# Two-block network on one core: query scaling, ready biases, early constants, a fourth weight buffer

## The chip, the cores and the metric

The kernel runs on one core of a Trainium2 chip, in one launch. The metric is the device time of an execution in microseconds. Most executions of one kernel agree within 0.3%.

## The reference

The input is 256 tokens of width 1024, one batch. The reference is two blocks of two layers each, all in float32.

- The first block. Layer 0: a norm, an input projection, a short causal convolution, a 4-head mLSTM and 4-head attention over 256 memory tokens, then an output projection and a gated feed-forward with a 3-tap convolution. Layer 1: 12-head banded attention with a table of relative biases, again with memory attention, output projection and feed-forward. It ends in a norm with the gain `final_g`.
- The second block. Each of its layers is modulated: `mod = silu(c) @ ada_w + ada_b` gives shifts, scales and gates. The even layer mixes 8-head neighbourhood attention over a grid with a bias table `rpb` (plus all 256 context keys) and HGRN2, a gated linear recurrence that runs in both directions. The odd layer is a gated short convolution. Each is followed by a feed-forward with 2816 hidden features; a norm ends it.

Every attention computes `softmax(scale * q k + bias)` with `scale = 64 ** -0.5 = 1/8`:

```
s = einsum('bqhd,bkhd->bhqk', qc, kc) * scale + bias
p = softmax(where(valid, s, -inf))
```

## The kernel before

**Layout and products.** Activations lie with features on the partitions, 8 tiles of 128 features by 256 tokens. Float32 products are made from two halves: each operand is split into a high part and the rest, and each 128 x 128 weight tile needs three matmuls (high x high, high x low, low x high: L122 to L124 in `mm3`). Down projections use a wider form (L129, L130 in `mm2`). A projection of 8 k tiles is 24 matmuls of 256 (or 258) columns.

**Weights.** `load_w` loads 512 KB into a raw tile (4 buffers `wraw`), through SyncE's queue; ScalarE casts the high half (L114), VectorE subtracts for the low half (L115), into one of 3 buffers `w`. `out_proj` runs 8 projections; where it is given a pool and two tags, its fourth weight (`nt == 3`) goes into two dead tiles of that pool instead (`wspare`). Before the change the two output projections of the second block do this and those of the first block don't.

**PSUM.** Projections rotate over five banks (`acc` 3, `sc` 2) in wide stages and over three in others; VectorE evacuates them, mostly times the norm's `rstd`. A norm is: a sum of squares, a product with ones, a power on GpSimd (`inv_rms`, L224), transposes that spread it (L218), and a copy to `rstd`.

**Order.** A planner orders the instructions of every engine with simulated times, taking ready work in program order; `issue_after` puts one instruction behind another in its engine's queue. Each engine, and SyncE's load queue, then runs its list in order. A pool that is closed gives its bytes to the next pool opened at the same place; in a pool with `reuse_waits="tile"` a tile waits for the readers and writers of the old tiles under it.

**Modulation.** 96 steps `ada` each load 512 KB and make one reduction on VectorE (L469; 16 of them two). `ada_after` puts a step behind an evacuation; `ada_done` forces those that are needed. The pair `rates` of a feed-forward gives a step after every so many up tiles, and how many after each down tile.

**Around the change.** `Pair.scores` makes the scores of two heads: L332 computes `(score + bias) * -0.125` and the running minimum, so the biases are made 8 times as large before: for the band on GpSimd at L883 after its load at L882; for the neighbourhood at L1177, with the window mask `win` added at L1179. At the entry to the second block's first mixer (`mix2`, from L943) the pool's constants for HGRN2 are made on GpSimd and VectorE: `reset` (L974, L975), the masks `mf` and `mk` (L981, L984), `decay` (L988), `win` (L1153 to L1158). Just before, x is multiplied by `final_g` (L938, 8 instructions), which only the evacuations of that mixer's output projection need. The kernel begins with 16 matmuls on ones (L262) and with the loads of `memx` and of the memory keys' weights (L272, L273).

Of the kernel before, what the change touches and what calls it, by code (L numbers as in the profile page):

```python
# [9 lines left out]
F32 = mybir.dt.float32  # L10
# [42 lines left out]
def network(ctx: ExitStack, tc: tile.TileContext, a):  # L53
# [205 lines left out]

    ps = bank("fil")  # L260
# [40 lines left out]
    class Pair:  # L301
# [7 lines left out]
        def scores(self):  # L309
# [6 lines left out]
            for qts in ((0, 1),) if one else ((0,), (1,)):  # L316
# [9 lines left out]
                for qt, j in [(qt, j) for qt in qts for j in range(2)]:  # L326
# [3 lines left out]
                    for lo, n, b in self.bias(j, qt):  # L330
# [3 lines left out]
                            scale=-0.125, scalar=3e38 if mn is None else mn, op0=ALU.add,  # L334
# [198 lines left out]
    with tc.tile_pool(name="mix0", bufs=1, reuse_waits="tile") as pool:  # L533
        def scaled(ps, out):
            nc.vector.tensor_tensor(out=out, in0=ps[:, :S], in1=rstd[:, :S], op=ALU.mult)

        cm = pool.tile([P, S], F32, name="cm")
# [5 lines left out]
        qk = pool.tile([P, 12, S], F32, name="qk")  # L543

        qz = pool.tile([P, 4, S], F32, name="qz")
        nc.gpsimd.memset(qz, 0.0)

        def qk_step(nt):
# [17 lines left out]
            return nc.scalar.activation(qk[:, nt], cv, AF.Silu)  # L566
# [77 lines left out]
        def lstm_scores(h):  # L644
# [3 lines left out]
            parts = ((own, qk[:, own]), (shared, qz[:, h]))  # L648
# [11 lines left out]
            for i, (kt, q) in enumerate(parts):  # L660
                nc.tensor.matmul(sp[:, :S], qk[:, 6 + kt, 0:P], q, start=i == 0, stop=i == 1)
            for i, (kt, q) in enumerate(parts):
                nc.tensor.matmul(sp[:, S:384], qk[:, 6 + kt, P:S], q[:, P:S],
                                 start=i == 0, stop=i == 1)
# [26 lines left out]
        def mem_q(nt):  # L691
            scaled(proj_fm(a["w_qm0"][nt], x2), qm[:, nt])
# [46 lines left out]
        out_proj(a["w_aout"], y2, (6, 7, 0, 1, 2, 3, 4, 5), evac)  # L739
# [42 lines left out]
    with tc.tile_pool(name="mix1", bufs=1, reuse_waits="tile") as pool:  # L782
        kk = pool.tile([P, 6, S], F32, name="kk")
        vv = pool.tile([P, 2, 768], F32, name="vvb")
        qq = pool.tile([P, 6, S], F32, name="qq")
# [77 lines left out]
        def q_step(nt):  # L863
            scaled(proj_fm(a["w_bq"][nt], x2), qq[:, nt] if nt < 6 else qm[:, nt - 6])

        def k_step(nt):
            scaled(proj_fm(a["w_kvk"][nt], kv2), kk[:, nt])
# [11 lines left out]
        def band_pair(pair):  # L879
            def prep():  # L880
                relb = pool.tile([P, 2, S], F32, tag="relb", bufs=2, name="relb")
                nc.gpsimd.dma_start(out=relb, in_=a["rel"][pair])  # L882
                nc.gpsimd.tensor_scalar(out=relb, in0=relb, scalar1=8.0, scalar2=1.0,  # L883
                                        op0=ALU.mult, op1=ALU.mult)
# [4 lines left out]
                pool, qq[:, pair],  # L889
                lambda nk: [(0, nk, kk[:, pair, :nk])],  # L890
# [23 lines left out]
        out_proj(a["w_bout"], y2, (6, 7, 0, 1, 2, 3, 4, 5), evac)  # L914
# [22 lines left out]
    for kt in range(KT):  # L937
        nc.vector.scalar_tensor_tensor(out=x[:, kt], in0=x[:, kt], scalar=col("final_g", kt),  # L938
                                       in1=rx[:, :S], op0=ALU.mult, op1=ALU.mult)

    NM = S + 2
    with tc.tile_pool(name="mix2", bufs=1, reuse_waits="tile") as pool:
# [30 lines left out]
        reset = pool.tile([P, 8, 32], F32, name="reset")  # L973
        nc.gpsimd.memset(reset, 1.0)  # L974
        nc.gpsimd.memset(reset[:, :, 0:1], 0.0)  # L975
        resetf = reset.rearrange("p a b -> p (a b)")

        mk = pool.tile([P, 2, 2, P], U8, name="mk")
        mf = pool.tile([P, 2, 2, P], F32, tag="at", bufs=2, name="mf")
        for d, sgn in ((0, 1), (1, -1)):  # L980
            nc.gpsimd.affine_select(out=mf[:, d, 0], in_=ones, compare_op=ALU.is_ge, fill=0.0, base=0,  # L981
                                    pattern=[[sgn, P]], channel_multiplier=-sgn)
            for tb in range(2):
                nc.vector.tensor_copy(mk[:, d, tb], mf[:, d, 0])  # L984


        decay = pool.tile([P, 4, 2, 5], F32, name="decay")
        nc.gpsimd.memset(decay, 1.0)  # L988
# [161 lines left out]


        win = pool.tile([P, 64], F32, name="win")
        nc.gpsimd.memset(win, 0.0)  # L1153
        for half in range(2):
            hs = slice(64 * half, 64 * half + 64)
            nc.gpsimd.affine_select(out=win[hs, 0:48], in_=win[hs, 0:48], compare_op=ALU.is_ge,
                                    fill=NEG, base=8, pattern=[[1, 48]], channel_multiplier=-1)
# [44 lines left out]
        with tc.issue_after(sigmoid.ins):  # L1202
            for head in heads:
                head.logs()
# [216 lines left out]
```

## Time and profile before

| what | us |
|---|---|
| median of the runs shown | 1366.92 |
| lowest | 1364.28 |
| highest (one run of three, far off the others) | 3344.76 |
| the profiled execution | 1365.22 |
| its span, first to last instruction | 1363.5 |
| TensorE busy in it | 1338.8 (98%) |
| VectorE busy | 1118.2 (82%) |
| ScalarE busy | 830.1 (61%) |
| GpSimd busy | 49.1 (4%) |
| mean granted TensorE clock | 0.997 of full speed |

PE is TensorE (PEld its weight loads), DVE VectorE, ACT ScalarE, POOL GpSimd, SPq SyncE's queue of loads. A matmul's end in the trace is modelled and overlaps the next one; the number of matmuls in a stretch says more than the busy time.

### The profile page before, as it was taken

The page shows a single profiled execution, that of the slowest core. Times are in us where ns is not written, and L with a number is a line of the kernel's source. Part 1 is how long each engine was busy: PE and PEld are TensorE (multiplying, and loading weights), DVE is VectorE, ACT ScalarE, POOL GpSimd, SP SyncE. Part 2 cuts the span into 40 slices and gives each one's busy share as a digit, 9 for nine tenths or more (in the row PEclk, how much of TensorE's full clock was granted, in tenths as well). Part 3 has the DMA queues.
Part 4 walks back from the last instruction along what each step waited for, and adds up shares of the span by engine and source line. Part 5 has one row for each costly group of instructions (what it writes and reads, how often), then busy time and mean ns, then how long its engine had stood idle before and what let it go on. Part 6 is the DMA issues. An engine that isn't in the chain of part 4 may idle for free.

```text
span 1363.5 us, 26870 instructions
## 1 busy us (share of the span) xinstructions
PE 1338.8 (98%) x10498; PEld 1282.0 (94%) x10498; DVE 1118.2 (82%) x2121; ACT 830.1 (61%) x1440; POOL 49.1 (4%) x72
## 2 busy tenths in 40 slices
PE   9999999999999999999999999999999999999997
PEld 8998999989999999999888987999998999999986
DVE  6887799997775968998988876699889898888854
ACT  6856655555567766555647766576654455666653
POOL 1000000000101000000040110000000000000000
PEclk9999999999999999999999999999999999999999
DMA  7753677766645657888875443467779876655563
GB/s 272 246 176 105 230 231 228 235 202 191 213 148 155 209 201 242 283 283 277 269 229 173 151 153 123 139 232 230 224 216 339 284 244 195 186 177 181 176 187 100
DMA packets 80352, 284.19 MB, mean 208 GB/s; under 512 B 8928, under 2 KB 10080, under 8 KB 80096
## 3 DMA queue, kind: packets, MB, share of 16 engines
q1 hardware_dynamic: 79136, 278.67, 63.9%
q0 software_dynamic: 800, 3.15, 0.7%
q8 instruction: 82, 1.34, 0.4%
q10 hardware_dynamic: 288, 0.66, 0.1%
q14 instruction: 46, 0.38, 0.1%
HBM read 281.39 MB, written 1.05 MB: 207 GB/s over the span
## 4 chain that ended last, share of the span: by engine, by line
PE 93%; DVE 3%; ACT 2%; issue 1%; DMA 0%; POOLq 0%; POOL 0%; DVEq 0%; SPq 0%; ACTq 0%
PE ps_acc L124 15%; PE ps_acc L122 15%; PE ps_acc L123 15%; PE ps_sc L124 7%; PE ps_sc L123 7%; PE ps_sc L122 7%; PE ps_acc L129 6%; PE ps_sc L129 4%; PE ps_acc L130 3%; PE ps_sc L130 2%; PE ps_sc L323 2%; PE ps_acc L154 2%; PE ps_acc L156 2%; PE ps_acc L155 2%; DVE w L115 1%
## 5 line engine op out<-in xcount | busy, mean ns | idle before, releaser
L114 ACT CAST w<-wraw 128x1024 fp32r<-128x1024 f32 (+3 forms) x434 | 443.5, 1027 | 390.3 <-PE ps_acc L124 146.3
L115 DVE TENSOR_TENSOR w<-wraw,w 128x1024 fp32r<-128x1024 f32 (+3 forms) x434 | 519.9, 1201 | 120.5 <-ACT w L114 117.2
L124 PE MATMUL ps_acc<-x,w 128*128 128x258 f32 (+1 forms) x1576 | 446.5, 285 | 2.1 <-DVE w L115 2.1
L122 PE MATMUL ps_acc<-x,w 128*128 128x258 f32 (+1 forms) x1576 | 444.8, 285 | 3.7 <-DVE ev L947 1.6
L123 PE MATMUL ps_acc<-x,w 128*128 128x258 f32 (+1 forms) x1576 | 446.3, 284 | 0.0
L122 PEld LDWEIGHTS ps_acc<-x,w 128*128 128x128 f32 x1576 | 298.5, 190 | 7.9 <-ACT w L114 2.4
L124 PEld LDWEIGHTS ps_acc<-x,w 128*128 128x128 f32 x1576 | 298.9, 190 | 3.9 <-DVE w L115 2.5
L123 PEld LDWEIGHTS ps_acc<-x,w 128*128 128x128 f32 x1576 | 299.3, 190 | 2.3 <-issue 2.0
L122 PE MATMUL ps_sc<-x,w 128*128 128x256 f32 (+1 forms) x824 | 232.6, 282 | 1.9 <-ACT w L114 1.1
L124 PE MATMUL ps_sc<-x,w 128*128 128x256 f32 (+1 forms) x824 | 233.2, 283 | 0.0
L123 PE MATMUL ps_sc<-x,w 128*128 128x256 f32 (+1 forms) x824 | 232.6, 283 | 0.0
L122 PEld LDWEIGHTS ps_sc<-x,w 128*128 128x128 f32 x824 | 156.0, 189 | 2.9 <-ACT w L114 1.5
L123 PEld LDWEIGHTS ps_sc<-x,w 128*128 128x128 f32 x824 | 155.6, 189 | 0.4 <-issue 0.4
L124 PEld LDWEIGHTS ps_sc<-x,w 128*128 128x128 f32 x824 | 155.9, 189 | 0.1
L129 PE MATMUL ps_acc<-a,w 128*128 128x512 f32 x352 | 123.0, 390 | 0.0
L469 DVE CUSTOM_DVE_ANT_0 ada<-ada,cvec,vec 128x1024 f32<-128x1024 f32 x96 | 121.9, 1278 | 0.8 <-DMA ada<-w_ada 0.7
L130 PE MATMUL ps_acc<-a,w 128*128 128x256 f32 x352 | 99.3, 282 | 1.3 <-DVE w L115 1.3
L129 PE MATMUL ps_sc<-a,w 128*128 128x512 f32 x264 | 92.5, 390 | 0.0
L408 DVE SCALAR_TENSOR_TENSOR cv<-g,vec,cv 128x255 f32<-128x255 f32 (+1 forms) x176 | 83.2, 477 | 0.4 <-ACT cv L406 0.3
L129 PEld LDWEIGHTS ps_acc<-a,w 128*128 128x128 f32 x352 | 66.0, 188 | 13.5
L130 PE MATMUL ps_sc<-a,w 128*128 128x256 f32 x264 | 74.5, 282 | 0.0
L130 PEld LDWEIGHTS ps_acc<-a,w 128*128 128x128 f32 x352 | 66.5, 189 | 2.3 <-DVE w L115 2.0
(382 smaller groups left out, 1910.8 us busy)
## 6 DMA issues: line engine op xcount, KB each, us to landing
wraw<-w_up SPq DMA_DIRECT2D x176, 512.0 KB, 4.3
ada<-w_ada SPq DMA_DIRECT2D x96, 512.0 KB, 4.7
wraw<-w_dn SPq DMA_DIRECT2D x64, 512.0 KB, 4.3
wraw<-w_ev SPq DMA_DIRECT2D x44, 512.0 KB, 3.8
wraw<-w_dn SPq DMA_DIRECT2D x32, 384.0 KB, 4.0
wraw<-w_od SPq DMA_DIRECT2D x24, 512.0 KB, 4.6
wraw<-w_qk SPq DMA_DIRECT2D x12, 512.0 KB, 4.6
wraw<-w_aout SPq DMA_DIRECT2D x8, 512.0 KB, 3.6
```

The costliest lines, as they stand in the source:

```text
L114: nc.scalar.copy(hi[:, c], raw[:, c])
L115: nc.vector.tensor_tensor(out=lo[:, c], in0=raw[:, c], in1=hi.bitcast(F32)[:, c], op=ALU.subtract)
L122: nc.tensor.matmul(ps, w.h[:, c], x.h[:, kt, :n], start=first, stop=False)
L123: nc.tensor.matmul(ps, w.h[:, c], x.l[:, kt, :n], start=False, stop=False)
L124: nc.tensor.matmul(ps, w.l[:, c], x.h[:, kt, :n], start=False, stop=last)
L129: nc.tensor.matmul(ps, w.h[:, c], x.both[:, :, kt, :n], start=first, stop=False)
L130: nc.tensor.matmul(ps[:, 0], w.l[:, c], x.h[:, kt, :n], start=False, stop=last)
L154: nc.tensor.matmul(ps, x.l[:, kt, t], v.h[:, c], start=kt == 0, stop=False)
L155: nc.tensor.matmul(ps, x.h[:, kt, t], v.h[:, c], start=False, stop=False)
L156: nc.tensor.matmul(ps, x.h[:, kt, t], v.l[:, c], start=False, stop=kt == 7)
L408: nc.vector.scalar_tensor_tensor(out=cv[:, so], in0=g[:, si], scalar=conv(i, ft), in1=cv[:, so], op0=ALU.mult, op1=ALU.add)
L469: nc.vector.tensor_tensor_reduce(out=out, in0=wt, in1=cvec[j], scale=1.0, scalar=col("ada_b", 48 * l + n), op0=ALU.mult, op1=ALU.add, accu ...
```

## The change

1. The factor 1/8 moves from the scores into the queries, as they are evacuated (`scaled_q`, `q_step`, `na_query`); L332 keeps only the sign.
2. The band's biases are used as loaded. The neighbourhood's window mask is put into the packed table on the host, so `win` and both GpSimd instructions on each bias tile go.
3. `reset`, `mk` and `decay` become constants that are made at the very beginning, `mf` in a pool of its own that is closed before the pool `mem` opens.
4. The output projections of the first block get a fourth weight buffer: the dead tiles `qz` and `qk0`, and `kk4` and `qq4`. For that `qk`, `kk` and `qq` are cut into tiles of 4 (and 2) parts.
5. The multiplication of x by `final_g` is traced after the logs of the HGRN2 heads.
6. The second block's first feed-forward has rates (2, 1) in place of (2, 2).

```diff
+    reset = const.tile([P, 8, 32], F32, name="reset")
+    mk = const.tile([P, 2, 2, P], U8, name="mk")
+    decay = const.tile([P, 4, 2, 5], F32, name="decay")
+    nc.gpsimd.memset(reset, 1.0)
+    nc.gpsimd.memset(reset[:, :, 0:1], 0.0)
+    nc.gpsimd.memset(decay, 1.0)
+    with tc.tile_pool(name="masks", bufs=1) as pool:
+        mf = pool.tile([P, 2, P], F32, name="mf")
+        for d, sgn in ((0, 1), (1, -1)):
+            nc.gpsimd.affine_select(out=mf[:, d], in_=ones, compare_op=ALU.is_ge, fill=0.0, base=0,
+                                    pattern=[[sgn, P]], channel_multiplier=-sgn)
+            for tb in range(2):
+                nc.vector.tensor_copy(mk[:, d, tb], mf[:, d])
 ...
-                            scale=-0.125, scalar=3e38 if mn is None else mn, op0=ALU.add,
+                            scale=-1.0, scalar=3e38 if mn is None else mn, op0=ALU.add,
 ...
+        def scaled_q(ps, out):
+            nc.vector.scalar_tensor_tensor(out=out, in0=ps[:, :S], scalar=0.125, in1=rstd[:, :S],
+                                           op0=ALU.mult, op1=ALU.mult)
 ...
-        qk = pool.tile([P, 12, S], F32, name="qk")
-        qz = pool.tile([P, 4, S], F32, name="qz")
+        qks = [pool.tile([P, 4, S], F32, tag=f"qk{i}", name="qk") for i in range(3)]
+        def qk(nt):
+            return qks[nt // 4][:, nt % 4]
+        qz = pool.tile([P, 4, S], F32, tag="qz", name="qz")
 ...
-            scaled(proj_fm(a["w_qm0"][nt], x2), qm[:, nt])
+            scaled_q(proj_fm(a["w_qm0"][nt], x2), qm[:, nt])
 ...
-        out_proj(a["w_aout"], y2, (6, 7, 0, 1, 2, 3, 4, 5), evac)
+        out_proj(a["w_aout"], y2, (6, 7, 0, 1, 2, 3, 4, 5), evac, pool, ("qz", "qk0"))
 ...
-            scaled(proj_fm(a["w_bq"][nt], x2), qq[:, nt] if nt < 6 else qm[:, nt - 6])
+            ps = proj_fm(a["w_bq"][nt], x2)
+            nc.vector.scalar_tensor_tensor(out=qq(nt) if nt < 6 else qm[:, nt - 6], in0=ps[:, :S],
+                                           scalar=0.125, in1=rstd[:, :S], op0=ALU.mult, op1=ALU.mult)
 ...
-                nc.gpsimd.tensor_scalar(out=relb, in0=relb, scalar1=8.0, scalar2=1.0,
-                                        op0=ALU.mult, op1=ALU.mult)
 ...
-        out_proj(a["w_bout"], y2, (6, 7, 0, 1, 2, 3, 4, 5), evac)
+        out_proj(a["w_bout"], y2, (6, 7, 0, 1, 2, 3, 4, 5), evac, pool, ("kk4", "qq4"))
 ...
-    for kt in range(KT):
-        nc.vector.scalar_tensor_tensor(out=x[:, kt], in0=x[:, kt], scalar=col("final_g", kt),
-                                       in1=rx[:, :S], op0=ALU.mult, op1=ALU.mult)
 ...
-        reset = pool.tile([P, 8, 32], F32, name="reset")
-        (and the rest of reset, mk, mf, decay, win as above)
 ...
+        def na_query(nt):
+            t = raw(nt)
+            nc.vector.tensor_scalar(out=nq[:, nt], in0=t[:, :S], scalar1=t[:, S : S + 1], scalar2=0.125,
+                                    op0=ALU.add, op1=ALU.mult)
 ...
-            na_steps += [lambda nt=nt: plus_shift(raw(nt), nq[:, nt]),
+            na_steps += [lambda nt=nt: na_query(nt),
 ...
-                nc.gpsimd.tensor_scalar(out=rv, in0=rv, scalar1=8.0, scalar2=1.0,
-                                        op0=ALU.mult, op1=ALU.mult)
-                nc.gpsimd.tensor_tensor(out=rv, in0=rv, op=ALU.add,
-                                        in1=win.unsqueeze(1).to_broadcast([P, 12, 64]))
 ...
             for head in heads:
                 head.logs()
+        for kt in range(KT):
+            nc.vector.scalar_tensor_tensor(out=x[:, kt], in0=x[:, kt], scalar=col("final_g", kt),
+                                           in1=rx[:, :S], op0=ALU.mult, op1=ALU.mult)
 ...
-    x2, ss = ffn2(0, gains[:, 2], (2, 2))
+    x2, ss = ffn2(0, gains[:, 2], (2, 1))
```

## Rows read from the trace of the kernel before

**Rows 1.** The page: engines' busy time, then the chain that ended last.
```profile
PE 1338.8 (98%) x10498; PEld 1282.0 (94%) x10498; DVE 1118.2 (82%) x2121; ACT 830.1 (61%) x1440; POOL 49.1 (4%) x72
...
PE 93%; DVE 3%; ACT 2%; issue 1%; DMA 0%; POOLq 0%; POOL 0%; DVEq 0%; SPq 0%; ACTq 0%
```

**Rows 2.** Stretches: length, busy time (count) of each engine, clock, DMA share, GB/s.
```profile
0.00:24.00 24.00, 20.91 (x137) 20.18 (x138) 16.33 (x40) 17.14 (x32) 0.49 (x5) 1.00 0.77 258
...
144.00:168.00 24.00, 24.00 (x206) 24.00 (x205) 17.21 (x30) 14.02 (x21) 1.98 (x3) 1.00 0.72 243
...
696.00:724.00 28.00, 25.23 (x194) 24.54 (x193) 22.35 (x39) 13.44 (x20) 14.73 (x20) 0.94 0.57 180
732.00:740.00 8.00, 6.62 (x55) 6.42 (x54) 8.00 (x18) 7.97 (x17) 0.00 (x0) 1.00 0.20 69
...
1016.00:1032.00 16.00, 14.71 (x85) 12.78 (x84) 14.18 (x23) 7.63 (x11) 0.00 (x0) 1.00 0.87 276
...
1150.00:1167.20 17.20, 17.20 (x148) 17.20 (x147) 16.75 (x30) 13.14 (x23) 0.00 (x0) 1.00 0.57 183
1167.20:1172.00 4.80, 4.80 (x42) 4.80 (x42) 0.52 (x3) 1.40 (x2) 0.63 (x1) 1.00 0.38 114
```

**Rows 3.** Instructions by line, GpSimd: count, busy us, mean ns, idle before.
```profile
L981 POOL TENSOR_SCALAR_AFFINE_SELECT mf<-ones 128x128 f32<-128x128 f32 x2 | 0.6, 303 | 0.0
...
L974 POOL MEMSET reset<- 128x256 f32 x1 | 0.3, 317 | 177.7 <-PE ps_sc L124 177.7
```

**Rows 4.** Timeline of the start: start us, us, engine, what [idle before it].
```profile
0.80 0.38 SPq L272 DMA_DIRECT2D memx<-memT  x1
...
5.65 0.80 PE L122 MATMUL ps_acc<-x,w 128*128 128x256 f32 x2 [0.75 <-ACT w L276]
```

**Rows 5.** Line L984, VectorE: ns min/median/max, first and last start.
```profile
L984 DVE CAST mk<-mf x4: 217/218/247, 701.4 to 702.2; 128x128 uint8<-128x128 f32 x4
```

**Rows 6.** Timeline, TensorE, near 21 us.
```profile
21.27 0.39 PE L154 MATMUL ps_acc<-w,x 128*128 128x264 f32 x1 [1.22 <-ACT memv L296]
```

**Rows 7.** Timeline, 135 to 139 us, first block's first output projection.
```profile
136.40 2.95 ACT L114 CAST w<-wraw 128x1024 fp32r<-128x1024 f32 x3 [2.44 <-PE ps_sc L124]
...
138.44 0.39 PE L122 MATMUL ps_acc<-x,w 128*128 128x256 f32 x1 [0.44 <-ACT w L114]
```

**Rows 8.** Timeline, 490 to 495 us, first block's second output projection.
```profile
492.02 2.95 ACT L114 CAST w<-wraw 128x1024 fp32r<-128x1024 f32 x3
```

**Rows 9.** Timelines: variance, subtraction, matmul and powers near 710; one power near 519.
```profile
705.57 0.16 DVE L211 TENSOR_SCALAR v<-ps_att 128x2 f32<-128x2 f32 x1 [2.81 <-PE ps_att L205]
705.71 2.56 DVE L115 TENSOR_TENSOR w<-wraw,w 128x1024 fp32r<-128x1024 f32 x1
...
708.33 0.39 PE L124 MATMUL ps_acc<-x,w 128*128 128x258 f32 x1 [0.69 <-DVE w L115]
...
711.76 2.81 POOL L224 TENSOR_TENSOR rt<-v,neghalf 128x2 f32<-128x2 f32 x2
...
519.21 0.73 POOL rt L224
```

**Rows 10.** Timeline, TensorE, 714 to 717 us.
```profile
714.62 0.43 PE L218 MATMUL ps_att<-ident,rt 128*128 128x128 f32 x2 [0.50 <-POOL rt L224]
716.63 0.47 PE L122 MATMUL ps_acc<-x,w 128*128 128x258 f32 x1 [1.57 <-DVE ev L947]
```

**Rows 11.** Stretch with the lower clock, columns as in rows 2.
```profile
718.00:720.00 2.00, 2.00 (x11) 2.00 (x11) 2.00 (x7) 0.15 (x1) 0.00 (x0) 0.50 0.65 252
```

**Rows 12.** Timeline, VectorE: x times final_g.
```profile
717.16 3.25 DVE L938 SCALAR_TENSOR_TENSOR x<-x,vec,rstd 128x256 f32<-128x256 f32 x8
```

**Rows 13.** Timeline near 1022 us, second block's first down projection.
```profile
1021.44 1.28 DVE L469 CUSTOM_DVE_ANT_0 ada<-ada,cvec,vec 128x1024 f32<-128x1024 f32 x1
...
1023.92 0.39 PE L130 MATMUL ps_acc<-a,w 128*128 128x256 f32 x1 [1.29 <-DVE w L115]
```

**Rows 14.** Line L469: the modulation's reductions.
```profile
L469 DVE CUSTOM_DVE_ANT_0 ada<-ada,cvec,vec x96: 1256/1278/1285, 87.0 to 1136.8; 128x1024 f32<-128x1024 f32 x96
```

**Rows 15.** Timeline, VectorE: first evacuation of the last output projection.
```profile
1150.31 0.48 DVE L1318 SCALAR_TENSOR_TENSOR x<-ps_acc,mod,x 128x256 f32<-128x256 f32 x1 [3.67 <-PE ps_acc L124]
```

More of the change, by code (lines that the diff above doesn't have):

```diff
@@ L565, in qk_step @@
                 return last
-            return nc.scalar.activation(qk[:, nt], cv, AF.Silu)
+            return nc.scalar.activation(qk(nt), cv, AF.Silu)
         v1 = pool.tile([P, 2, 4 * 193], F32, name="v1")
@@ L647, in lstm_scores @@
                            else (h // 2 * 3 + 2, h // 2 * 3 + 1))
-            parts = ((own, qk[:, own]), (shared, qz[:, h]))
+            parts = ((own, qk(own)), (shared, qz[:, h]))
             mb = bank("att")
@@ L660, in lstm_scores @@
             for i, (kt, q) in enumerate(parts):
-                nc.tensor.matmul(sp[:, :S], qk[:, 6 + kt, 0:P], q, start=i == 0, stop=i == 1)
+                nc.tensor.matmul(sp[:, :S], qk(6 + kt)[:, 0:P], q, start=i == 0, stop=i == 1)
             for i, (kt, q) in enumerate(parts):
-                nc.tensor.matmul(sp[:, S:384], qk[:, 6 + kt, P:S], q[:, P:S],
+                nc.tensor.matmul(sp[:, S:384], qk(6 + kt)[:, P:S], q[:, P:S],
                                  start=i == 0, stop=i == 1)
@@ L782, in network, with kk, qq @@
     with tc.tile_pool(name="mix1", bufs=1, reuse_waits="tile") as pool:
-        kk = pool.tile([P, 6, S], F32, name="kk")
+        heads6 = {n: [pool.tile([P, k, S], F32, tag=f"{n}{k}", name=n) for k in (4, 2)]
+                  for n in ("kk", "qq")}
+        def kk(pair):
+            return heads6["kk"][pair // 4][:, pair % 4]
+        def qq(pair):
+            return heads6["qq"][pair // 4][:, pair % 4]
         vv = pool.tile([P, 2, 768], F32, name="vvb")
-        qq = pool.tile([P, 6, S], F32, name="qq")
         qm = pool.tile([P, 2, S], F32, name="qm1")
@@ L888, in band_pair @@
             p = Pair(
-                pool, qq[:, pair],
-                lambda nk: [(0, nk, kk[:, pair, :nk])],
+                pool, qq(pair),
+                lambda nk: [(0, nk, kk(pair)[:, :nk])],
                 lambda kb, j: vv[:, kb, (2 * pair + j) * 64 : (2 * pair + j + 1) * 64],
@@ L970, in network @@
         nv = pool.tile([P, 2, 512], F32, name="nv")
-        reset = pool.tile([P, 8, 32], F32, name="reset")
-        nc.gpsimd.memset(reset, 1.0)
-        nc.gpsimd.memset(reset[:, :, 0:1], 0.0)
         resetf = reset.rearrange("p a b -> p (a b)")
[L978 to L988, printed above, removed]
         class Head:
@@ L1147, in readout @@
                 split(y2, 4 + h, og, col("hg_norm_w", h))
[L1152 to L1157, printed above, removed]
-            nc.gpsimd.affine_select(out=win[hs, 16:64], in_=win[hs, 16:64], compare_op=ALU.is_ge,
-                                    fill=NEG, base=7 - 16, pattern=[[-1, 48]], channel_multiplier=1)
         def na_value(nt):
@@ L1397, in _pack @@
     c, kc, r = np.arange(64)[:, None, None], np.arange(64)[None, None, :], np.arange(6)[None, :, None]
-    rpb = np.stack([pad[:, 5 - half + r, 63 + kc - c] for half in range(2)], axis=1)
+    inside = (kc >= np.clip(c - 8, 0, 48)) & (kc < np.clip(c - 8, 0, 48) + 16)
+    rpb = np.stack([np.where(inside, pad[:, 5 - half + r, 63 + kc - c], np.float32(NEG))
+                    for half in range(2)], axis=1)
     out["rpb"] = rpb.reshape(4, 2, P, 6, 64).transpose(0, 2, 1, 3, 4)
```

3 lines of the change are left out of this document (1 added, 2 removed).

## The prediction

> **What bounds the kernel now.** I read the share of each engine first, then the chain of waits, then the span cut into stretches, then TensorE's idle gaps one by one. TensorE is busy 1338.8 of 1363.5 us and the chain that ended last is 93% TensorE [rows 1]: all idle together is 24.7 us, so no edit that leaves the matmuls alone can bring more than that and what a lowered clock costs. The change takes no matmul away. The pitch of a full stretch is 24.00 us / 206 = 0.1165 us a matmul; one projection of 24 is 2.8 us. Against that pitch the stretches with too few matmuls show where something else ends last [rows 2]: the start (137 in 24 us), the two output projections that get a fourth buffer (around 120 to 140 and 480 to 495 us), the entry to the third mixer (HGRN2; 194 in 28 us, clock 0.94), and the second block's first down projection (85 in 16 us). Most of VectorE's and ScalarE's work lies beside TensorE and costs nothing; it matters where one of their results is the last to arrive. VectorE has no room in 732 to 740 (8.00 of 8.00) and in 1150 to 1167.2 (16.75 of 17.20), and that is where the change puts work.
>
> The profiled execution took 1365.22 us (span 1363.5, 1.7 around it); the median shown is 1366.92 and the lowest 1364.28. I make the sum against 1365.22 and take a median of 1365 to 1367 as the same thing.
>
> **Start: +1.8.** The masks are built in a small pool that is closed just before the pool with memx opens, so mf and memx share bytes, and the first load of the kernel (issued at 0.80 us, [rows 4]) must now wait until mf is last read. In front of that, GpSimd gets two memsets of the reset tile, one of decay and two selects: 0.317 + 0.135 + 0.141 + 2 x 0.303 = 1.20 us [rows 3], behind the identity's select (1.14 to 1.43 us): 2.63 us. Two of the four 0.217 us copies [rows 5] follow the second select: about 3.1 us, so memx may leave 2.3 us later. SyncE issues in order: if it keeps the order, the first weights, memv, vec and x behind memx are 2.3 us late too, and TensorE's first product, at 5.65, comes at about 8. If the planner lets the weight loads pass, memx arrives behind four more of them, TensorE starts some 3 us late, but x is not late, and the 1.22 us that TensorE waits at 20.05 [rows 6] takes part of it back. TensorE also runs at half clock from 5.65 to 10.27 (0.215 us a matmul, 21 of them, 2.1 us lost), which a longer gap may prolong by as much. Below: 0, if the pools don't share bytes. Above: 2.3 + 2.1 = 4.4. I take 1.8, between 3 - 1.22 and 2.3.
>
> **Fourth buffer in the first block's output projections: -1.7 and -1.2.** Three projections run side by side over the k tiles as they become ready, end together, and free their three weight buffers together. At 136.40 ScalarE starts three casts, the first product of the next projection comes at 137.49 and that of the one after at 138.44 [rows 7]; from 136.67 to 138.78 TensorE does 4 matmuls (0.47 us) in 2.11: 1.64 lost. With the fourth set converted earlier there are 24 more matmuls, 2.8 us, which covers the casts (1.05 + 1.2). Twelve instead of nine matmuls for a k tile also fill a little of the gaps between 123 and 127 (1.0 us in all). -1.7, between 0 and -2.6. The extra cast (1.05 us on ScalarE, 1.23 on VectorE) moves ahead, to 108 to 122 us, and qz, qk0 are dead by then (last scores near 100 us). The second one shows the same three casts at 492.02 [rows 8]: 492.45 to 494.41 holds 4 matmuls, 1.5 lost, less some transposes that were there anyway: -1.2, between 0 and -1.6.
>
> **Constants, biases and masks off GpSimd at 696 to 724: -4.2.** GpSimd is busy 14.73 of these 28 us [rows 2], in front of the power that makes the norm's scale: the first variance is ready at 705.57, the powers start at 711.76 and take 2.81 for two, against 0.73 for one at 519.21; beside GpSimd's work one 1.23 us subtraction took 2.56 and TensorE waited 0.69 [rows 9]. The scale comes so late that TensorE's five banks fill: gaps of 0.50 and 1.57 [rows 10]. Then the granted clock is at the lower of its two levels, 0.50 from 718 to 720 [rows 11], and back soon after 720; 17 matmuls at 0.215 cost 1.7. Together 0.69 + 0.50 + 1.57 + 1.7 = 4.5. Without that work the scale is there near 710, before the fifth bank is full; I leave 0.3 for the two norms that remain. Bounds: -5.2 (44 matmuls short of 28 us at 0.1176) and -1.6. The 8 multiplications of x by final_g (3.25 us, [rows 12]) are traced behind the logs; VectorE has idle time between the forget projections, so I take 0, with 3.25 as the upper end.
> By the Trainium skill (SBUF — State Buffer, Who interferes with whom) a VectorE instruction with two SBUF inputs and a GpSimd one that reads SBUF hold the shared ports one at a time; the 2.56 agrees. By that rule the powers still queue behind subtractions of 1.23 and the 0.50 gap stays: -3.7.
>
> **The pace of the modulation, (2, 2) to (2, 1): -1.3, then +1.4.** From 1020.24 two reductions of 1.28 stand in front of a weight's subtraction, and TensorE waits 1.29 [rows 13]; with one, the subtraction is 1.28 earlier. 1020 to 1032 is also ten matmuls short: -1.3, between 0 and -1.7. All 96 steps are still wanted: 89 are done by the end of this stage now, 81 after. Each of the eight steps of the fourth mixer (the gated convolution) then still takes one, and 7 are left for the evacuations of the last output projection, which has none now. 7 x (1.278 + 0.082) = 9.5 us go onto VectorE [rows 14] where 0.45 us is free up to 1167.2 and 4.28 in the next 4.8 us [rows 2]. Three evacuations come together at 1150.31 with the next casts behind them [rows 15], the same pattern as at 1020: I put that wait at 1.4, between 0 and 9.5.
>
> **The 1/8 in the queries, ready biases: 0.** Ten evacuations of queries become the form with a scalar (0.06 us more each), four shifts go from ScalarE to VectorE, and GpSimd loses 6 x 1.01 and 4 x (1.12 + 2.29) us. The chain has nearly no GpSimd in it [rows 1]. TensorE's projections hide the rest; if the cover goes, 4 x 0.35 + 0.6 = 2 us. The bias loads still go by GpSimd's queue, with nothing behind them now. From -0.9 to +2.
>
> Sum: 1.8 - 1.7 - 1.2 - 4.2 - 1.3 + 1.4 = -5.2, so 1360.0 us.
>
> **Rivals.**
> (1) Gains eaten at the ends: the start costs 4.4 and the extra buffers bring half, because VectorE has no time for a fourth conversion earlier: 1360 + 2.6 + 1.5 = 1364. For it: VectorE is above 90% busy in places before both projections. Against: three raw weights are converted ahead there already. Chance 0.2.
> (2) Slower: the seven reductions in 1150 to 1172. VectorE needs 2.6 us a projection there (1.22 + 0.48 + 0.48 + 0.42) and 3.96 with a reduction, against TensorE's 2.8; the slack of two projections less a cast, 3.3 us, is gone after the third, and from there each reduction holds back a subtraction that TensorE waits for. Whole price 9.5 in place of 1.4: 1368. For it: the wait in [rows 13]. Against: the planner may leave reductions to the 4.28 free us. Chance 0.1.
> (3) x times final_g lands in 732 to 740, where VectorE is full and TensorE already waits 1.37: 1363. Chance 0.1.
> (4) The change at the start doesn't do what I read in it (the pools don't share bytes, or the wait is hidden by 20.05): 1358, and 1356 if the last projection takes its reductions for nothing. Chance 0.1.
> The forecast itself, 1357.5 to 1362.5, has 0.5.
>
> **Numbers.** The range 1354 to 1368 takes in the forecast, rivals 1, 3 and 4, the bounds on the entry to the mixer, and the edge of rival 2; about 0.15 stays outside, most of it above. 2% is 27 us, about what can be told from no change here. TensorE's idle time is 24.7 us in all, so faster by more is next to excluded (0.01); slower by more would need a planner's accident, 0.02.
>
> **What would show it.** The first load's issue and TensorE's first product (8 against 5.65); no casts that TensorE waits for near 136 and 492 and an extra weight tile there; 696 to 724 with clock 1.00 and some 235 matmuls, the first power right behind v; no wait of 1.29 near 1020, and the reductions among the evacuations near 1150 with a wait before a subtraction. I would be wrong if TensorE's matmul count in 696 to 724 stays near 194, or if the starts agree.

## The result, and the profile after

The changed kernel takes **1378.41 us** (median of 6 runs, 1376.76 to 1379.17), the kernel before 1365.38 beside it: ratio 1.0092 [1.0082, 1.0103], 13.0 us slower. The forecast was 1360.0, 1354 to 1368: it said faster, and the kernel is slower, in either case by less than 2%. The profiled execution took 1376.99 us (span 1375.3).

The page's first rows and its chain (as in [rows 1]) show TensorE still at 98%, GpSimd with 20 us less work, and 91% instead of 93% of the chain on TensorE.

```profile
PE 1343.0 (98%) x10498; PEld 1285.7 (93%) x10498; DVE 1113.0 (81%) x2125; ACT 832.5 (61%) x1437; POOL 28.7 (2%) x53
...
PE 91%; DVE 4%; issue 2%; DMA 1%; ACT 1%; POOL 0%; SPq 0%; POOLq 0%; DVEq 0%
```

To see where 11.8 us of span went I took TensorE's **position**: the matmuls of both traces counted from the start (weighted by columns), and the time at which each has done the same amount. It is worked out from the timeline, not a view of the profile. Both traces have 10498 matmul records, one of which is 0.12 us at full pace, so a figure is good to some tenths of a microsecond. It compares one trace of each kernel; how far two traces of one kernel lie apart is said where it matters.

| stretch, us of before | predicted | found |
|---|---|---|
| start, 0 to 118 | +1.8 | +2.1 |
| first block, first output projection, 118 to 144 | -1.7 | -0.2 |
| first block, second output projection, 480 to 545 | -1.2 | **+8.1** |
| entry to HGRN2, 696 to 732 | -4.2 | -4.8 |
| 732 to 744 | 0 | +2.6 |
| 744 to 864 | 0 | -0.3 |
| second block's feed-forward, 1020 to 1080 | -1.3 | -2.2 |
| last output projection, 1150 to 1185 | +1.4 | **+6.2** |
| sum | -5.2 | +11.5 |

The stretches of the kernel after (columns as in [rows 2]): few matmuls and a clock under 1.00 at 492 and 528, too few at 1152 and 1176, and 99 at the entry to HGRN2.

```profile
0.00:24.00 24.00, 18.20 (x122) 17.68 (x123) 16.11 (x41) 16.11 (x31) 1.43 (x10) 1.00 0.72 256
492.00:504.00 12.00, 7.95 (x45) 6.31 (x44) 7.62 (x13) 5.33 (x11) 0.00 (x0) 0.75 0.31 94
528.00:540.00 12.00, 10.20 (x72) 9.77 (x71) 6.72 (x13) 7.19 (x14) 0.00 (x0) 0.86 0.39 132
708.00:720.00 12.00, 11.84 (x99) 11.64 (x98) 8.64 (x17) 5.30 (x8) 4.29 (x5) 1.00 0.63 212
1016.00:1032.00 16.00, 15.91 (x92) 13.85 (x91) 11.39 (x18) 7.20 (x10) 0.00 (x0) 1.00 0.71 218
1152.00:1164.00 12.00, 9.98 (x80) 9.37 (x79) 7.98 (x14) 5.59 (x10) 0.00 (x0) 1.00 0.61 174
1176.00:1188.00 12.00, 9.93 (x80) 9.42 (x79) 10.19 (x21) 5.17 (x8) 1.75 (x1) 1.00 0.51 161
```

Three of the same stretches of the kernel before:

```profile
492.00:504.00 12.00, 11.10 (x91) 10.65 (x91) 11.97 (x21) 9.41 (x17) 0.00 (x0) 1.00 0.71 271
708.00:720.00 12.00, 9.60 (x64) 9.11 (x65) 11.01 (x19) 5.48 (x9) 6.49 (x4) 0.87 0.68 220
1176.00:1188.00 12.00, 12.00 (x101) 12.00 (x100) 10.66 (x21) 9.42 (x17) 0.00 (x0) 1.00 0.69 216
```

**Around 496 us.** VectorE after, timeline (start, length, what, idle before it). L166 is the split of an attention output, which the output projection reads; L486 the modulation's reduction (L469 before).

```profile
487.97 1.29 DVE L486 CUSTOM_DVE_ANT_0 ada<-ada,cvec,vec 128x1024 f32<-128x1024 f32 x1 [2.64 <-DMA ada<-w_ada]
...
490.46 0.42 DVE L166 TENSOR_TENSOR x<-ps_att,x 128x256 fp32r<-128x256 f32 x1
493.01 1.28 DVE L486 CUSTOM_DVE_ANT_0 ada<-ada,cvec,vec 128x1024 f32<-128x1024 f32 x1 [2.14 <-DMA ada<-w_ada]
...
495.08 1.28 DVE L486 CUSTOM_DVE_ANT_0 ada<-ada,cvec,vec 128x1024 f32<-128x1024 f32 x1 [0.78 <-DMA ada<-w_ada]
...
498.08 1.28 DVE L486 CUSTOM_DVE_ANT_0 ada<-ada,cvec,vec 128x1024 f32<-128x1024 f32 x1 [1.70 <-DMA ada<-w_ada]
...
499.29 0.42 DVE L166 TENSOR_TENSOR x<-ps_att,x 128x256 fp32r<-128x256 f32 x1
```

The last split is behind three reductions, each of which waits in VectorE's order for its row of weights to land. In the kernel before no reduction stands between 486 and 499 us and the splits run at 486.08 and 490.61. TensorE after, timeline of its waits:

```profile
499.76 0.58 PE L123 MATMUL ps_acc<-x,w 128*128 128x256 f32 x1 [3.65 <-DVE x L166]
...
533.16 0.71 PE L885 MATMUL ps_fil<-hv,ckt 128*128 128x128 f32 x4 [1.19 <-ACT ckt L881]
534.48 0.39 PE L122 MATMUL ps_acc<-x,w 128*128 128x256 f32 x1 [0.61 <-DVE g L414]
```

Why the reductions came earlier is seen in SyncE's queue. Before, six loads of w_bout hold it from 468.56 for 26.13 us; the rows of the modulation come at 494.74:

```profile
468.56 26.13 SPq L109 DMA_DIRECT2D wraw<-w_bout  x6
494.74 0.90 SPq L465 DMA_DIRECT2D ada<-w_ada  x2
```

After, with a fourth converted set to free the raw buffers, they hold it for 11.83, and five rows go out from 481.99:

```profile
470.11 11.83 SPq L109 DMA_DIRECT2D wraw<-w_bout  x6
481.99 12.68 SPq L482 DMA_DIRECT2D ada<-w_ada  x5
```

**The last output projection.** VectorE after, timeline: reductions between the first three evacuations (L1324), the weight's subtraction L115 behind them.

```profile
1156.20 0.48 DVE L1324 SCALAR_TENSOR_TENSOR x<-ps_acc,mod,x 128x256 f32<-128x256 f32 x1 [4.02 <-PE ps_acc L124]
1156.61 1.27 DVE L486 CUSTOM_DVE_ANT_0 ada<-ada,cvec,vec 128x1024 f32<-128x1024 f32 x1
...
1157.81 0.48 DVE L1324 SCALAR_TENSOR_TENSOR x<-ps_sc,mod,x 128x256 f32<-128x256 f32 x1
1158.20 1.27 DVE L486 CUSTOM_DVE_ANT_0 ada<-ada,cvec,vec 128x1024 f32<-128x1024 f32 x1
...
1159.41 0.48 DVE L1324 SCALAR_TENSOR_TENSOR x<-ps_acc,mod,x 128x256 f32<-128x256 f32 x1
1159.81 1.21 DVE L115 TENSOR_TENSOR w<-wraw,w 128x1024 fp32r<-128x1024 f32 x1
```

TensorE then waits for that subtraction, and at the end for the norm's power behind the last evacuations:

```profile
1161.07 0.39 PE L124 MATMUL ps_acc<-x,w 128*128 128x256 f32 x1 [1.33 <-DVE w L115]
...
1184.61 0.43 PE L218 MATMUL ps_att<-ident,rt 128*128 128x128 f32 x2 [1.31 <-POOL rt L224]
```

### The profile page after: what moved, and what is told of

It is laid out like the page before. It is cut to its first block, busy times and chain, and to the rows that moved or that the text cites. A ratio compares the mean times of both kernels' runs of the same rounds, so it can differ in the third digit from the quotient of the medians.

```text
span 1375.3 us, 26870 instructions
## 1 busy us (share of the span) xinstructions
PE 1343.0 (98%) x10498; PEld 1285.7 (93%) x10498; DVE 1113.0 (81%) x2125; ACT 832.5 (61%) x1437; POOL 28.7 (2%) x53
## 4 chain that ended last, share of the span: by engine, by line
PE 91%; DVE 4%; issue 2%; DMA 1%; ACT 1%; POOL 0%; SPq 0%; POOLq 0%; DVEq 0%
PE ps_acc L124 15%; PE ps_acc L122 15%; PE ps_acc L123 14%; PE ps_sc L124 7%; PE ps_sc L123 7%; PE ps_sc L122 7%; PE ps_acc L129 6%; PE ps_sc L129 4%; PE ps_acc L130 3%; PE ps_sc L130 2%; PE ps_sc L340 2%; PE ps_acc L154 2%; PE ps_acc L155 2%; PE ps_acc L156 2%; DVE w L115 1%
## 5 line engine op out<-in xcount | busy, mean ns | idle before, releaser
L115 DVE TENSOR_TENSOR w<-wraw,w 128x1024 fp32r<-128x1024 f32 (+3 forms) x432 | 513.5, 1192 | 130.5 <-ACT w L114 127.7
L122 PE MATMUL ps_acc<-x,w 128*128 128x256 f32 (+1 forms) x1568 | 444.6, 285 | 8.5 <-ACT x L292 4.7
L123 PE MATMUL ps_acc<-x,w 128*128 128x256 f32 (+1 forms) x1568 | 445.8, 285 | 3.7 <-DVE x L166 3.7
L124 PE MATMUL ps_acc<-x,w 128*128 128x256 f32 (+1 forms) x1568 | 445.9, 286 | 2.1 <-DVE w L115 2.1
L486 DVE CUSTOM_DVE_ANT_0 ada<-ada,cvec,vec 128x1024 f32<-128x1024 f32 x96 | 122.3, 1277 | 7.3 <-DMA ada<-w_ada 7.3
```

Source lines behind the costliest of these rows:

```text
L115: nc.vector.tensor_tensor(out=lo[:, c], in0=raw[:, c], in1=hi.bitcast(F32)[:, c], op=ALU.subtract)
L122: nc.tensor.matmul(ps, w.h[:, c], x.h[:, kt, :n], start=first, stop=False)
L123: nc.tensor.matmul(ps, w.h[:, c], x.l[:, kt, :n], start=False, stop=False)
L124: nc.tensor.matmul(ps, w.l[:, c], x.h[:, kt, :n], start=False, stop=last)
L486: nc.vector.tensor_tensor_reduce(out=out, in0=wt, in1=cvec[j], scale=1.0, scalar=col("ada_b", 48 * l + n), op0=ALU.mult, op1=ALU.add, accu ...
```

## The experiments

Theory from the two traces: the fourth buffer in the second output projection (8.1) and the pace (6.2 - 2.2) make the loss, the start 2; the rest is as predicted. Where a kernel is called "after", its edit is made to the kernel after.

**The second output projection.** Three buffers there again:

```diff
-        out_proj(a["w_bout"], y2, (6, 7, 0, 1, 2, 3, 4, 5), evac, pool, ("kk4", "qq4"))
+        out_proj(a["w_bout"], y2, (6, 7, 0, 1, 2, 3, 4, 5), evac)
```

> The changed kernel with three weight buffers in the first block's second output projection. Theory: the fourth buffer frees SyncE's queue earlier, the modulation's loads and their reductions come ahead of the last pair's split on VectorE, which stands behind loads; without it the 8.1 us lost between 480 and 545 us are regained: 1370.3 us, splits ahead of reductions, the old waits of about 0.9 us near 492 back. Rival: the loss comes from the shift of the whole stage (the earlier scores, the biases), and the fourth buffer saves its 1.2 us: 1379.6.

Measured 1369.54, ratio to before 1.0026 [1.0017, 1.0035]: 8.9 less than after. TensorE's position gains 8.0 across 488 to 552, from 0.6 behind after to 7.4 ahead, and keeps it. Its stretches have the matmuls back:

```profile
492.00:504.00 12.00, 11.01 (x90) 10.07 (x87) 9.96 (x18) 9.15 (x18) 0.00 (x0) 1.00 0.49 185
528.00:540.00 12.00, 12.00 (x105) 12.00 (x104) 11.01 (x21) 8.11 (x13) 0.00 (x0) 1.00 0.70 220
```

The buffer kept, the eight reductions of the context's states taken out (they run later), pace (2, 2):

```diff
             last = nc.vector.tensor_tensor(out=sgc[:, i], in0=sgc[:, i], in1=lfc[:, i], op=ALU.mult)
-            ada_after(last)
...
-    x2, ss = ffn2(0, gains[:, 2], (2, 1))
+    x2, ss = ffn2(0, gains[:, 2], (2, 2))
```

> The changed kernel with its fourth buffer in both output projections, but no modulation step behind the context states; the eight steps are taken by the pace (2, 2) later, so that from the gated convolution on the counts are those of the changed kernel. Theory: with no reduction in front of the last pair's split the 8.1 us between 480 and 545 go although the fourth buffer stays, the 2.2 us of the second block's first down projection come back as a loss, and the loss near 1155 stays: 1372.5 us. Rival: the fourth buffer's own casts and its four projections side by side cost the 8.1: 1380.6.

Measured 1375.09, 1.0069 [1.0051, 1.0087], 2.6 above the theory; 5.4 is gained at the projection, not 8.1. The wait for a split is gone, those of 1.19 and 0.61 behind the projection are not:

```profile
492.00:504.00 12.00, 10.94 (x85) 9.38 (x84) 7.92 (x16) 9.30 (x20) 0.00 (x0) 1.00 0.25 86
528.00:540.00 12.00, 10.18 (x82) 9.78 (x83) 10.36 (x21) 7.28 (x14) 0.00 (x0) 1.00 0.42 132
```

The last context state is asked for behind the projection (`fill.rest()`). Asking for it ahead:

```diff
+        fill.rest()
         out_proj(a["w_bout"], y2, (6, 7, 0, 1, 2, 3, 4, 5), evac, pool, ("kk4", "qq4"))
-        fill.rest()
```

> After, with the rest of the context's states asked for ahead of the second output projection instead of behind it; the fourth buffer and the reductions stay. Theory (the loss at 480 to 545 is two things: splits held up by reductions at 500, about 5.3, and the last context state left behind the projection, 2.8 at 528 to 536): 1375.6, the waits of 1.19 and 0.61 near 532 gone, the wait of 3.65 near 500 still there. Rival (the later loss only follows from the earlier one): 1378.4, or both waits change together.

Measured 1371.18, 1.0032 [1.0017, 1.0046]: 7.2 less than after, 4.4 under my theory. Both waits went; the position gains 8.1 from 480 to 560 (and loses 3.4 again in the last output projection, of which below). VectorE's order moved the reductions ahead of the last scores, and the last split waits for nothing but ScalarE's half:

```profile
489.23 1.29 DVE L486 CUSTOM_DVE_ANT_0 ada<-ada,cvec,vec 128x1024 f32<-128x1024 f32 x1 [0.83 <-DMA ada<-w_ada]
...
490.90 0.42 DVE L166 TENSOR_TENSOR x<-ps_att,x 128x256 fp32r<-128x256 f32 x1
495.65 0.42 DVE L166 TENSOR_TENSOR x<-ps_att,x 128x256 fp32r<-128x256 f32 x1 [4.33 <-ACT x L165]
```

So the theory of two separate losses falls: one edit to where the states are asked for removes both.

**The pace.** After with (2, 2), the last two lines of the diff before the previous one, alone:

> The changed kernel with the pace (2, 2) again. Theory: the seven reductions that moved among the last output projection's evacuations cost the 6.2 us that the changed kernel loses against the kernel before between 1150 and 1185 us, and the two down projections' steps gave 2.2: net 4.0 less, 1374.4 us, no wait before a subtraction near 1155, and the 1.29 us wait near 1020 back. Rival: the loss near 1155 comes from the planner's other order there (the pace is not its cause); then 1380.6, that is the 2.2 lost again and nothing regained.

Measured 1371.80, 1.0041 [1.0026, 1.0056], 6.6 less than after, where the theory had 4.0. By position the last output projection gives back 6.4 and the down projections lose 2.3, 4.1 together, as said; the medians give more because the trace of after is of an execution of 1376.99, under its median of 1378.41 (see the last section). No wait is left from 1152 to 1176 (80 and 97 matmuls in after):

```profile
1152.00:1164.00 12.00, 12.00 (x105) 12.00 (x104) 7.64 (x15) 7.02 (x13) 0.00 (x0) 1.00 0.46 164
1164.00:1176.00 12.00, 12.00 (x103) 12.00 (x102) 10.11 (x19) 6.50 (x12) 0.00 (x0) 1.00 0.68 214
```

**The start.** First the mask tile in bytes of its own, in the pool of constants; then, in another run, the whole block of reset, mk and decay back in the third mixer as in the kernel before:

```diff
-    with tc.tile_pool(name="masks", bufs=1) as pool:
-        mf = pool.tile([P, 2, P], F32, name="mf")
+        mf = const.tile([P, 2, P], F32, name="mf")
```

> The changed kernel with the masks' scratch tile among the constants, so it shares no bytes with memx. Theory: the first load leaves near 0.8 us again and the first product comes near 5.65 instead of 9.59; at 24 us and after, the changed kernel was 2.0 us late, so 1376.4 us. Rival: the late start is GpSimd's and VectorE's work itself in front of the first products, not the shared bytes; then the first product stays near 9.6 and the time at 1378.4.

> After, with reset, masks and decay built inside the third mixer as in the kernel before; the bias additions on GpSimd stay removed. Theory (the start cost 2.0 and the entry to the mixer gained by the 13.6 us of bias and window work, not by these 1.2 us of constants): 1376.4, start as in before (first product near 5.65), 696 to 732 within 0.8 of after. Rival A (the constants are what stood ahead of the powers at the entry): 1378.4 - 2.0 + 4.8 = 1381. Rival B (what is won at the start is given back later, as in the run with the mask tile apart): 1378.4.

Measured 1379.14 and 1377.54, ratios 1.0091 [1.0076, 1.0106] and 1.0074 [1.0056, 1.0093]. TensorE starts at 6.84 and 5.39 instead of 9.59 and is 1.4 and 1.9 ahead of after at 24 us. The first is only 0.4 ahead from 60 us on; the second stays about 2 ahead, through the entry to HGRN2 too (104 matmuls from 708 to 720). Neither median is the 1376.4 of the theories: both lose 3.7 to 3.8 more than after in the last output projection, where VectorE's order came out a little different, and in the second run one of the reductions there waits 1.60 us for its row at 1170. So the price of that stage isn't one number: by position it is 6.3 to 10.6 in the nine traces that have these reductions there, 6.3 to 7.9 in the four with after's order on VectorE and 7.9 to 10.6 in the five with another. Stretches of the second:

```profile
708.00:720.00 12.00, 12.00 (x104) 12.00 (x103) 7.17 (x15) 4.47 (x5) 2.99 (x3) 1.00 0.69 234
1164.00:1176.00 12.00, 9.11 (x73) 8.47 (x71) 10.40 (x19) 5.60 (x9) 0.00 (x0) 1.00 0.81 270
```

**Two parts that should do nothing.** The final_g loop at its old place (behind `rx = rstd_of(v1)`), and three buffers in the first output projection:

```diff
-        for kt in range(KT):
-            nc.vector.scalar_tensor_tensor(out=x[:, kt], in0=x[:, kt], scalar=col("final_g", kt),
-                                           in1=rx[:, :S], op0=ALU.mult, op1=ALU.mult)
...
-        out_proj(a["w_aout"], y2, (6, 7, 0, 1, 2, 3, 4, 5), evac, pool, ("qz", "qk0"))
+        out_proj(a["w_aout"], y2, (6, 7, 0, 1, 2, 3, 4, 5), evac)
```

> After, with the eight multiplications of x by final_g back ahead of the third mixer. Theory (they ran in VectorE's idle time at 720 to 726 and are not what TensorE waits for near 741): 1378, within 0.7, and the gap of 2.46 us near 741 stays; at most 0.5 is lost where they stand at the entry, 700 to 712. Rival (the moved multiplications delay what TensorE waits for near 741): 1375.8, the gap near 741 is gone or near 1.4.

> After, with three weight buffers again in the first of the two output projections alone. Theory (the wait was moved from 136.5 to 141.5, the gain is given back within 4 us): 1378.4, within 0.7; the curve of delay against after is 0 beyond 145 us, with a bulge of about 1.7 at 140. Rival (the prediction: the fourth buffer saves 1.7): 1380.1, the bulge stays.

Measured 1377.47 and 1378.99, both medians as the theories say (the second one's trace, of an execution of 1380.87, loses 10.6 in the last output projection). The multiplications run at 720.5 to 723.3, in after at 720.5 to 723.6: where they stand in the text doesn't set their place. The first output projection has 90 matmuls from 132 to 144 us with four buffers (after), with three (the second run) and before; by position the fourth is worth 0.2.

**Together.** After with three of these edits: the constants in the mixer, three buffers in the second output projection, the pace (2, 2):

> After, with three parts undone together: constants inside the third mixer, three weight buffers in the second output projection, pace (2, 2); left are the 1/8 in the queries, the ready biases, the moved multiplications and the fourth buffer in the first output projection. Theory (the parts add up): 1378.4 - 2.0 - 8.8 - 4.5 = 1363, between the 3.7 and 6.6 that the pace gave; under the 1365.4 of before. Rival (TensorE's time is given back at the next wait, as it was in the first output projection and after 732 us): 1366 to 1368, no better than before.

Measured 1363.87, 0.998 [0.9971, 0.999]; once more, beside the last version below, 1363.19, 0.9982 [0.9973, 0.9991]. That is 14.5 less than after; one by one the three gave 8.9, 6.6 and 0.9 by medians, 16.4 together, or 8.0, 4.1 and 1.9 by position, 14.0 together; by position the two traces of this kernel are 11.4 and 14.2 ahead of after. So they add up to within 2 to 3 us. Four variations of it: three buffers in the first output projection too, half the logarithms (diff below; the run leaves out four of the eight, with a scaled copy in their place), the early constants with bytes of their own, and final_g at its old place:

```diff
-        nc.scalar.activation(lfout, sg, AF.Ln, scale=lb[:, 1, i : i + 1], bias=lb[:, 0, i : i + 1])
+        if i < 4:
+            nc.scalar.activation(lfout, sg, AF.Ln, scale=lb[:, 1, i : i + 1], bias=lb[:, 0, i : i + 1])
+        else:
+            nc.vector.tensor_scalar(out=lfout, in0=sg, scalar1=-0.05, scalar2=-0.01, op0=ALU.mult,
+                                    op1=ALU.add)
```

> The kernel with three parts undone (1363.87), and with three weight buffers in the first output projection as well, so that no projection has a fourth. Theory (the fourth buffer moves the wait and gives nothing): 1363.9 to 1364.5. Rival (the prediction: it saves 1.7): 1365.6.

> The kernel with three parts undone, and four of the eight logarithms of the HGRN2 gates replaced by a scaled copy on VectorE (that part of the result is left out): ScalarE's block between two weight casts falls from 4.05 to 2.03 us. Theory (TensorE's wait of 2.47 near 735 is this block, standing ahead of a cast; the time won at the entry is given back here): the wait is below 0.8 and the end 1.5 to 2.5 earlier, 1361.4 to 1362.4. Rival (the casts are late for another reason, or VectorE's subtraction is late next): the wait is 1.5 or more, or another takes its place, 1363.4 to 1364.

> The kernel with three parts undone, but with the HGRN2 constants built at the very beginning as in after, their mask tile in bytes of its own. Theory (what was lost at the start is the shared bytes and the first weights' landing; 1.2 us less GpSimd work at the entry gives nothing): 1364.0 to 1365.5, first product near 6.8. Rival (early constants save their 1.2 us of GpSimd work at 700 to 715): 1362.5.

> The kernel with three parts undone, and the multiplications of x by final_g at their old place ahead of the third mixer: of the whole change only the 1/8 in the queries, the ready biases (no bias work on GpSimd) and the fourth buffer in the first output projection are left. Theory (the entry's gain is GpSimd's bias and window work alone): 1363.9, within 0.7; TensorE has over 95 matmuls in its 12 us from 708. Rival (3.25 us of VectorE work ahead of the norm scale delays the entry): 1365 to 1367.

Measured 1364.13, 1363.50, 1364.19 and 1363.43, all within 0.5 of it. The run with half the logarithms missed its theory (1361.4 to 1362.4): the wait near 735 became longer and moved to VectorE's subtraction, in an order that the new copies had changed:

```profile
734.09 1.22 DVE L115 TENSOR_TENSOR w<-wraw,w 128x1024 fp32r<-128x1024 f32 x1
```

The early constants' first product came at 5.42, not 6.84, with 1.18 of waiting at 10.52 for another weight. Which weight is late differs from trace to trace, and with it the start: at 60 us ten traces whose kernels start as before does, that of before among them, lie 0 to 2.0 us behind it, and the kernel with three parts undone 2.0 in one trace and 0.5 in the other.

**Does the predicted 1.2 exist?** Three edits of the kernel with three parts undone, all from diffs shown: the fourth buffer put back alone; with it `fill.rest()` ahead and no `ada_after(last)` in the states; with it `fill.rest()` ahead and all reductions kept.

> The kernel with three parts undone (1363.87), with nothing but the fourth weight buffer in the second output projection put back. Theory (the buffer by itself lets SyncE's queue reach the modulation rows 12.8 us earlier and so puts reductions ahead of the splits): 7.3 to 8.9 slower, 1371.2 to 1372.8, with a wait of over 3 us before L123 near 494 on a split. Rival (it takes the pace (2, 1) or the start's delay as well): within 3 of 1363.9.

> The kernel with three parts undone (1363.87), with the fourth weight buffer in the second output projection again, the reductions taken out of the eight context states, and the rest of these states asked for ahead of the projection. To be read by TensorE's position against the kernel with three parts undone up to 560 us, since the eight reductions left out there run in the last output projection at 1150 and cost up to 6 us there. Theory (without the two hindrances the fourth buffer saves the 1.2 of the prediction): 0.8 to 1.6 us ahead at 560; end 1363 to 1370. Rival (the wait only moves to the end of the four projections, as in the first output projection): 0 to 0.5 ahead or behind.

> A version put together from what held: after with the constants inside the third mixer, the pace (2, 2), and the fourth weight buffer in both output projections, the rest of the context's states asked for ahead of the second one, all reductions kept. Theory (the buffer's 1.1 is kept, and the reductions, now ahead of the last scores, don't hold up a split): 1362.3 to 1363.3, 0.6 to 1.5 under the kernel with three buffers beside it. Rival (the reductions cost elsewhere what the buffer gives): 1363.5 to 1365, no better than that kernel.

> The kernel with three parts undone once more, as the measure for the version beside it: 1363.9, within 0.7; 1.5 to 3 under before.

Measured 1371.06 (1.0035 [1.0023, 1.0047]), 1370.44 (1.0029 [1.0017, 1.0041]) and 1363.04 (0.9974 [0.9965, 0.9983]). The buffer alone costs 7.2 by medians and 8.2 by position, through the same queue and the same late split:

```profile
469.90 11.82 SPq L109 DMA_DIRECT2D wraw<-w_bout  x6
481.77 12.59 SPq L469 DMA_DIRECT2D ada<-w_ada  x5
```

Unhindered it gains 0.9 by position from 480 to 560 (predicted 1.2), and the reductions that then run at 1150 to 1190 cost 7.9 there. With all reductions kept it gains 0.8 by position in that stretch and 0.15 by medians, which the runs don't tell from nothing (the theory had 0.6 to 1.5). This last version and the one with three buffers are both faster than the kernel before, by 3.4 and 3.2 us.

## Why the prediction was wrong

**The step that failed: "Fourth buffer in the first block's output projections: -1.7 and -1.2".** The second is worth +8.1. I costed the extra conversion on ScalarE and VectorE and asked which tiles were dead, but not what stood in SyncE's queue behind the six loads: the modulation's rows, held back till 494.74 because raw buffers came free slowly. The fourth set freed the queue by 482; VectorE's order, made ahead of time, then put reductions before the last splits. Five rows in 12.68 us, of which the reductions waited 2.64, 2.14, 0.78 and 1.70 us, turned 1.28 us instructions into a block in front of a 0.42 us one. That the order followed from the queue is read from these rows; no run frees the queue without the buffer. The buffer alone shows it, and the position of the states decides it. About 2.5 of the 8.1 is TensorE's clock behind the waits (an estimate): between 480 and 560 after has 46 matmuls at the half pace of 0.215 us and before 21, and 25 x 0.0985 = 2.5; the granted clock is 0.75 and 0.86 in the two stretches above. The first one is worth 0.2 because four projections that end together wait for casts as three did: ScalarE's three casts moved from 136.40 [rows 7] to 140.80.

**Mis-sized: the pace, "-1.3, then +1.4".** The wait of 1.29 [rows 13] is gone and 1016 to 1032 holds 92 matmuls for 85. Seven reductions ran among the evacuations, as I said, and the last one of the mixer just ahead of them, at 1150.56; they cost 6.3 to 10.6 us. That is the mechanism of rival 2 (whole price 9.5, chance 0.1): I spread the slack of the first projections over them, but two stand among the first three evacuations, where [rows 15] had shown three coming together with the casts behind. By itself it would have moved the forecast by 5 to 9 us.

**The start: the way right, the size not settled.** +1.8 said, +2.1 found, by the second of my two ways: the weight loads pass, memx goes out at 2.89 instead of 0.80 [rows 4], TensorE starts at 9.59 instead of 5.65, and the wait of [rows 6] is gone. That the two figures agree is partly luck: the trace of before has the earliest start of the ten that begin as it does. At 60 us these ten lie 1.0 behind it on average, the seven with after's start 2.0 (1.3 to 2.7), so the price is nearer 1.0. No run has this start alone on the kernel with three parts undone. The half clock that I read at the start is a reading of the pace (0.215 us a matmul), while the granted clock of the profile says 1.00 from 0 to 24 us [rows 2]; after, that pace ends near 13.2, 3.7 us behind the first product against 4.6 before, so nothing was prolonged.

```profile
0.81 1.97 SPq L290 DMA_DIRECT2D wraw<-w_memk  x4
2.89 1.34 SPq L289 DMA_DIRECT2D memx<-memT  x3
...
9.59 0.80 PE L122 MATMUL ps_acc<-x,w 128*128 128x256 f32 x2 [4.68 <-ACT x L292]
```

**Right: the entry to HGRN2**, -4.2 said, -4.8 found: clock 1.00 instead of 0.87 in its 12 us, 99 matmuls instead of 64, and the power 0.76 behind the variance (6.2 before, [rows 9]). Of those 6.2 GpSimd's own queue made only the last 1.6: the second variance, which the powers need, was ready at 710.18, because VectorE had put subtractions in front of it, one of them the slow one of 2.56. The constants and final_g have no part in the gain: with the constants back in the mixer it is 5.1 by position, and 5.1 again with final_g at its old place too.

```profile
714.86 0.16 DVE L211 TENSOR_SCALAR v<-ps_att 128x2 f32<-128x2 f32 x1 [3.00 <-PE ps_att L205]
715.47 2.41 DVE L115 TENSOR_TENSOR w<-wraw,w 128x1024 fp32r<-128x1024 f32 x2
...
715.62 2.83 POOL L224 TENSOR_TENSOR rt<-v,neghalf 128x2 f32<-128x2 f32 x2 [6.15 <-DVE v L965]
```

The two powers still take 2.83, beside two subtractions of 2.41 together and with nothing else on GpSimd, against 0.73 for one power alone [rows 9]. That agrees with the rule of the Trainium skill that I had weighed (SBUF — State Buffer, Who interferes with whom: a VectorE instruction with two SBUF inputs and a GpSimd one that reads SBUF hold the shared ports one at a time). But of the 0.50 gap that I let stay by it 0.16 is left, so -3.7 was too little.

**Given back and not foreseen:** 2.6 us at 732 to 744. TensorE, earlier by the entry's gain, meets a weight cast at 742.60, which stands behind ScalarE's eight logarithms, another cast, a table load and three exponentials:

```profile
743.68 0.58 PE L122 MATMUL ps_acc<-x,w 128*128 128x258 f32 x1 [2.46 <-ACT w L114]
```

Before, TensorE waits 1.38 at this place, so the wait itself gives back 1.1. The other 1.5 is the granted clock right behind it. In the run with three buffers in the second output projection the same cast makes TensorE wait 2.47, but the clock stays at 1.00 and the stretch gives back 1.1 in all. The six us around the end of that wait, in after and then in that run:

```profile
743.00:749.00 6.00, 5.32 (x30) 5.14 (x32) 5.04 (x14) 4.54 (x10) 0.00 (x0) 0.72 0.68 214
```

```profile
735.70:741.70 6.00, 5.33 (x41) 4.82 (x42) 5.86 (x19) 5.93 (x12) 0.00 (x0) 1.00 0.66 219
```

Rival 3 had 3 us here, but for final_g's multiplications, which did nothing. Whether the logarithms or VectorE behind them bounds this stretch stays open: halving the former brought the latter forward.

**Right: the 1/8 and the ready biases** cost nothing visible; with the moved multiplications and the fourth buffer of the first output projection they are what is left of the change in the faster version with three buffers.

## What to carry to other kernels

Giving one stage another buffer releases the queue that fed it: before costing it, list what is next in that queue, who consumes it on an in-order engine, and what stands behind that consumer. A gain in front of a fixed block of work (here logarithms and exponentials) is partly given back there, and a wait can cost more than its length when the granted clock is lower behind it. A price read from one pair of traces wants a second trace of each kernel before it is called right. Work put off to a later stage must be costed at the place where its evacuations bunch, not by the stage's mean slack.

## What the runs showed that was not expected

The same waits didn't always cost the same clock: gaps of 0.25, 0.44 and 1.3 us near 1158 left the granted clock at 1.00 in the kernel after, and at 0.90 over the same 12 us in the run with final_g at its old place:

```profile
1152.00:1164.00 12.00, 9.98 (x71) 9.37 (x70) 8.74 (x15) 5.58 (x10) 0.00 (x0) 0.90 0.62 199
```

So 9 matmuls of that stretch hang on what the clock did and not on the order of the work; by position the stage costs 1.5 more in that run. The executions of the kernel after show the same: the two with a mean granted clock of 0.993 took 1376.8 and 1377.0 us, the four with 0.989 to 0.990 took 1378.3 to 1379.2. And the kernel with three parts undone, run twice, has 35 matmuls at 0.74 in one trace and 45 at 1.00 in the other from 842 to 848 us, and the two traces move 1.0 us apart there:

```profile
842.00:848.00 6.00, 5.32 (x35) 4.09 (x34) 4.51 (x15) 4.99 (x12) 0.00 (x0) 0.74 0.54 176
```

```profile
842.00:848.00 6.00, 5.33 (x45) 3.91 (x44) 3.46 (x14) 4.98 (x11) 0.00 (x0) 1.00 0.59 178
```

What decides it these runs don't show.
